# A trunk layer on one core: order of the x tiles, place of the gate row, and the filling of stick-breaking

## The chip, the core and the metric

The kernel runs on one core of a Trainium2 chip. The metric is device time in microseconds of one execution. Engines are named as in the profile: TensorE (PE, with its weight loads as PEld), VectorE (DVE), ScalarE (ACT), GpSimd (POOL) and SyncE (SP), whose queue issues the DMAs of this kernel.

## The reference

One layer with D = S = 1024, batch 1, float32. `h` feeds three groups of heads (mLSTM: 4 heads of 96; sliding window: 6 heads of 64 with 2 key/value heads; stick-breaking: 4 heads of 64), and their gated results go through `w_out`:

```python
mod = c_act @ w_mod + b_mod                       # c_act = silu(c)
shift, scale, gate = jnp.split(mod, 3, axis=-1)
h = rmsnorm(x, g_pre) * (1.0 + scale) + shift
proj = h @ w_in
(mu, mv, mi, mf, mz, aq, ak, av, az, sq, sk, sv, sz) = jnp.split(proj, OFFSETS, axis=-1)
y_m = mlstm_branch(mu, mv, mi, mf, ...) * silu(mz)
y_a = swa_branch(aq, ak, av, a_sinks) * silu(az)
y_s = stickbreak_branch(sq, sk, sv) * silu(sz)
y = concatenate([y_m, y_a, y_s]) @ w_out
x + gate * rmsnorm(y, g_post)
```

Stick-breaking, for queries `t` and keys `s < t`: `a = exp(log_sigmoid(z) + suffix)`, where `suffix` sums `log_sigmoid(-z)` over the keys between `s` and `t`, and the result is `a @ v`.

## The kernel before

Each large float32 product is made of three matmuls: both factors are split into a high part (rounded to the format that TensorE takes at full rate) and a low rest, and high x high, high x low and low x high are summed. Names with `h` and `l` at the end (`hh`/`hl`, `wh_d`/`wl_d`, `ah`/`al`) are such parts; ScalarE mostly makes the high part (a cast) and VectorE or GpSimd the low one (a subtraction).

The stages, in the order of TensorE:

- **x tiles** (0 to 34 us). Eight tiles of 128 tokens. For each, `x_sq` squares and sums on ScalarE (`junk`), `x_var` makes 1/rms (VectorE, then GpSimd, `rstd`), `x_scale` scales the tile, and `x_turn` transposes it on TensorE (`xps`, two groups of four) and copies the groups to `xT`. `mod_rows(k)` multiplies `silu(c)` with the modulation weights of one k slice (`mr`), `mod_sum(k)` turns the row into columns (`mps`, `sh`, `sc`), `mod_h(k, n)` makes `hh` and `hl` for one half of the tokens, and `mu_w(k)` splits a slice of the `mu` weights (`wmuh`, `wmul`).
- **mu** (22 to 72): `mu_mm(k, n)`, nine matmuls for one slice k of D and one half n of the tokens. The first, (0, 0), stands between the x tiles; from (0, 1) on they follow each other.
- **ptmif** (72 to 106): projection to the mLSTM's values and gates, by tokens.
- **gate chain** (106 to 151): `gmps` multiplies the two query and key matrices of the mLSTM (`wqk_s`) into one; then a chain of small transposes (`gtr`) with VectorE and ScalarE work between them (`fx`, `cm`, `mp`, `em`, `tcol`). Between the transposes, `fill(n)` issues n matmuls of the projections that are due anyway: `pd`, a transposed projection with weights `w_d` (48 matmuls to a tile of outputs), and `ptav`, the sliding window's values (24 to a tile of tokens, `vsh`/`vsl`, stored to `d_v`). `GF` holds the four counts, and `fill.through(I_AQ)` issues all that is left of `ptav`.
- **the gate row**: `gate_row` computes `gacc`, 32 instructions on VectorE over eight loads of 512 KB (`wg`, two buffers); `gate_sum` sums it over the partitions on TensorE (`gbps`, two halves) and writes the row `gbc`, which only the last stage of the kernel reads.
- **mLSTM** (about 175 to 244), chunk by chunk, with `cuh` (the convolution's result by heads), `mbc` (stabilizers, broadcast by a DMA), `qps`/`q`/`q1`, `kps` and `sps` (the scores).
- **sliding window** (244 to 331), with keys `ka` and values `va` loaded back from memory.
- **stick-breaking** (331 to 452): 40 steps `(h, pair, g)`; each transposes (`s_t`, tile `tp`), issues `SF[1]` fill matmuls on average, and three steps later multiplies with the values (`s_pv`, tile `ops`, one bank for the two quads of a head). `z`, `sg`, `pr` are the scores, the factors and their running products; `ys` collects the result.
- **the last projections and w_out** (452 to 569).

The order on TensorE is that of the code. For the x tiles the other engines and SyncE too follow the code; from the first slices of `mu` on a scheduler orders them, with the priorities that `tc.high_priority` gives. PSUM for fills has two banks, so a `ptav` tile can start when the evacuation of the tile before the last is done. At most eight DMAs of SyncE are under way: each waits for the landing of the one eight places ahead of it.

Of the kernel before, what the change touches and what calls it, by code (L numbers as in the profile page):

```python
# [13 lines left out]
ALU = mybir.AluOpType  # L14
# [17 lines left out]
C_CW, C_CB, C_NG, C_SKIP, C_SINK = 32, 44, 47, 50, 53  # L32
NCOLS = 59

EVD = (0, 1, 2, 3, 4)
WPRI, EPRI = 400, 200
GF = (48, 48, 48, 20)
PM = 12
MF = (12, 5, 5, 4)
AF_ = (4, 5, 4)  # L40
NPOOL = 3
SF = (6, 6.6, 2)
SL = 3
SGB = 8

# [2 lines left out]
def trunk(ctx: ExitStack, tc, x, w_ss, w_gate, rows, cols, w_mu, w_mif, w_dm, w_av, wqk, bif, alibi, w_out,  # L48
# [98 lines left out]
    def x_sq(i):  # L147

        junk = xp.tile([P, D], F32, tag="junk", bufs=1, name=f"junk{i}")
        ss, v, r = (sp.tile([P, 1], F32, tag=z, bufs=4, name=f"{z}{i}") for z in ("ss", "var", "rstd"))  # L150
        A.activation(junk, xt_[i], AF.Square, accum_out=ss)
        xs_[i] = (ss, v, r)

    def x_var(i):
        ss, v, r = xs_[i]
        V.tensor_scalar(out=v, in0=ss, scalar1=1.0 / D, scalar2=EPS, op0=ALU.mult, op1=ALU.add)
        G.tensor_tensor(out=r, in0=v, in1=mhalf[:, 0:1], op=ALU.pow)

    def x_scale(i):
        if i == NT - 1:  # L160
            A.mul(xt_[i], xt_[i], xs_[i][2])
        else:
            V.tensor_scalar(out=xt_[i], in0=xt_[i], scalar1=xs_[i][2], scalar2=None, op0=ALU.mult)

    def x_turn(i):
        for g in range(2):
            ps = sps.tile([P, 512], F32, tag="b", name=f"xps{i}_{g}")
            for q in range(4):
                k = g * 4 + q
                T.transpose(ps[:, q * P:(q + 1) * P], xt_[i][:, k * P:(k + 1) * P], ident)  # L170
            dst = xT[:, g * 4:(g + 1) * 4, i * P:(i + 1) * P]
            src = ps.rearrange("p (a b) -> p a b", a=4)
            if g == 1 and i in EVD:
                V.tensor_copy(dst, src)
            else:
                A.copy(dst, src)
# [74 lines left out]
    V.tensor_tensor(out=csil, in0=csil, in1=col[:, C_C:C_C + KT], op=ALU.mult)  # L251
    V.tensor_copy(csil32, csil.unsqueeze(2).to_broadcast([P, KT, 32]))
    V.tensor_scalar(out=col[:, C_BSC:C_BSC + KT], in0=col[:, C_BSC:C_BSC + KT], scalar1=1.0, scalar2=None, op0=ALU.add)
    x_sq(0)
    x_var(0)
    x_sq(1)
    x_scale(0)
    x_var(1)
    for i in range(NT):
        if i == 4:  # L260
            mod_rows(0)
            mod_sum(0)
            mod_h(0, 0)
        if i + 1 < NT:
            x_scale(i + 1)
        if i + 2 < NT:
            x_sq(i + 2)
            x_var(i + 2)
        if i == 4:
            mu_w(0)  # L270
        x_turn(i)
        if i == 4:
            mod_load(3)
            mu_load(3)
            mu_mm(0, 0)
        if i == NT - 2:
            mod_rows(1)
    mod_h(0, 1)
    mu_w(1)
    xstk.close()  # L280
    tw_stk = ExitStack()
    tw = pool("tw", side="right", stack=tw_stk)
# [244 lines left out]
    def gate_row():  # L527
        gacc = gp_.tile([P, D], F32, name="gacc")
        rowb = gp_.tile([P, 2, D], F32, name="rowb")
        load(rowb, rows.partition_broadcast(P))  # L530
        for s_ in range(4):
            a = gacc[:, s_ * 256:(s_ + 1) * 256]
            for q in range(2):
                w = gp_.tile([P, 4, 256], F32, tag="wg", bufs=2, name=f"wg{s_}_{q}")
                load(w, w_gate[s_][:, 4 * q:4 * q + 4, :])
                for i in range(4):
                    c = csil[:, 4 * q + i:4 * q + i + 1]
                    if q + i == 0:
                        V.tensor_scalar(out=a, in0=w[:, 0, :], scalar1=c, scalar2=None, op0=ALU.mult)
                    else:  # L540
                        V.scalar_tensor_tensor(out=a, in0=w[:, i, :], scalar=c, in1=a, op0=ALU.mult, op1=ALU.add)  # L541
# [125 lines left out]
    def m_qk(c):  # L667
# [5 lines left out]
        A.copy(d["q1"], heads(qps[0:MD, :], MH))
# [518 lines left out]
```

## Time and profile before

| | us |
|---|---|
| runs | 572.18, 572.54, 575.24 (median 572.54) |
| profiled execution | 571.31 |
| its span | 569.5 |
| TensorE busy | 533.2 (94%) |
| VectorE busy | 342.4 (60%) |
| ScalarE busy | 252.1 (44%) |
| GpSimd busy | 222.0 (39%) |

The mean granted clock of TensorE is 0.975. In 40 equal slices of 14.2 us, the profile gives the busy share of TensorE and the clock, both in tenths:

```profile
PE   4899999499997999999999999999999899999995
PEclk9699999989999999999999998999999999999998
```

The dips are the x tiles (slices 1 and 2), the stretch around 107 (slice 8), the entry of the mLSTM (slice 13) and the beginning and end of stick-breaking. In a row of the timeline stand the start, the duration, the engine, the line, the operation with its output and inputs, a count, and in brackets how long the engine stood idle before it and what ended that. In a row of windows stand the stretch, its length, the busy time (and instructions) of TensorE, its weight loads, VectorE, ScalarE and GpSimd, the granted clock, the DMA share and GB/s. In a list of waits stand the total, the number of times and the longest.

### The profile page before, as it was taken

What the parts mean: (1) busy time and instruction counts of PE and PEld (TensorE: products, weight loads), DVE (VectorE), ACT (ScalarE), POOL (GpSimd) and SP (SyncE); (2) the same over time, 40 slices, a digit from 0 to 9 for tenths busy, and PEclk for the clock granted to TensorE, in tenths of its full rate; (3) what the DMA queues carried; (4) which work ended last, traced back from release to release, by engine and by line L of the source; (5) the groups of instructions that cost most, each with busy time, mean ns of one, the idle gap of its engine ahead of it and who ended that gap; (6) DMA issues with size and microseconds to landing.
All of it is one profiled execution on the core that took longest, in us unless ns stands there. A gap on an engine that the chain in (4) does not pass through costs nothing.

```text
span 569.5 us, 8566 instructions
## 1 busy us (share of the span) xinstructions
PE 533.2 (94%) x2953; PEld 455.7 (80%) x2953; DVE 342.4 (60%) x768; ACT 252.1 (44%) x575; POOL 222.0 (39%) x208
## 2 busy tenths in 40 slices
PE   4899999499997999999999999999999899999995
PEld 3577799489996999888788777888888788888884
DVE  4467599664213677759888568786878443107232
ACT  5554433133012332336787677676766442104110
POOL 2344877321103243405534356566747253101000
PEclk9699999989999999999999998999999999999998
DMA  8973282545366945579964368548221369305421
GB/s 310 374 251 121 58 313 75 160 149 157 85 150 192 231 135 166 150 181 292 260 193 149 103 169 220 185 118 242 76 73 56 103 238 389 139 1 197 173 74 74
DMA packets 63659, 96.57 MB, mean 170 GB/s; under 512 B 17600, under 2 KB 36992, under 8 KB 63488
## 3 DMA queue, kind: packets, MB, share of 16 engines
q1 hardware_dynamic: 63616, 96.03, 53.7%
q8 instruction: 23, 0.38, 0.3%
q14 instruction: 20, 0.16, 0.1%
HBM read 69.24 MB, written 25.20 MB: 166 GB/s over the span
## 4 chain that ended last, share of the span: by engine, by line
PE 68%; DVE 12%; ACT 6%; DMA 5%; issue 4%; SPq 2%; POOL 2%; DVEq 0%; POOLq 0%; ACTq 0%
PE pd L360 22%; PE mu L237 6%; PE ptav L386 6%; PE op L1109 5%; PE op L1108 5%; PE op L1107 5%; DVE cu L508 3%; ACT zb L846 3%; SPq L65 2%; PE tp L993 2%; DVE gacc L541 2%; DMA xt<-in_x_dram 2%; DVE zb L856 2%; PE z L962 1%; PE ops L1012 1%
## 5 line engine op out<-in xcount | busy, mean ns | idle before, releaser
L360 PE MATMUL pd<-hh,wh_d 128*128 128x512 f32 x256 | 71.9, 407 | 0.0
L360 PE MATMUL pd<-hh,wl_d 128*128 128x512 f32 x256 | 71.7, 402 | 0.0
L360 PE MATMUL pd<-hl,wh_d 128*128 128x512 f32 x256 | 71.1, 402 | 0.0
L360 PEld LDWEIGHTS pd<-hh,wh_d 128*128 128x128 f32 x256 | 47.6, 194 | 8.3
L360 PEld LDWEIGHTS pd<-hl,wh_d 128*128 128x128 f32 x256 | 46.9, 191 | 8.4
L360 PEld LDWEIGHTS pd<-hh,wl_d 128*128 128x128 f32 x256 | 46.5, 190 | 8.2
L1107 PE MATMUL op<-woh,hh 128*128 128x512 f32 x128 | 50.6, 396 | 0.0
L1108 PE MATMUL op<-woh,hl 128*128 128x512 f32 x128 | 50.6, 396 | 0.0
L1109 PE MATMUL op<-wol,hh 128*128 128x512 f32 x128 | 50.6, 396 | 0.0
L303 POOL TENSOR_TENSOR wl_d<-w_d,wh_d 128x512 fp32r<-128x512 f32 x32 | 44.8, 1422 | 14.4 <-ACT wh_d L301 12.1
L981 POOL TENSOR_TENSOR sg<-sg,pr 128x512 f32<-128x512 f32 (+1 forms) x32 | 33.1, 1038 | 25.5 <-DVE pr L979 21.4
L72 DVE TENSOR_TENSOR al<-tp,ah 128x512 fp32r<-128x512 f32 (+2 forms) x56 | 27.6, 495 | 20.5 <-ACT ah L71 20.3
L856 POOL TENSOR_SCALAR zb<-zb,mx 128x256 f32<-128x256 f32 (+1 forms) x24 | 21.6, 911 | 41.9 <-DVE mx L853 11.3
L71 ACT CAST ah<-tp 128x512 fp32r<-128x512 f32 (+2 forms) x56 | 24.4, 436 | 28.0 <-PE tp L993 21.6
L1120 ACT ACTIVATE sj<-op 128x512 f32<-128x512 f32 x16 | 9.5, 598 | 61.3 <-PE op L1109 58.8
L1124 POOL TENSOR_TENSOR st<-st,mhalf 128x1 f32<-128x1 f32 x8 | 4.4, 554 | 67.3 <-DVE st L1123 44.9
L1108 PEld LDWEIGHTS op<-woh,hl 128*128 128x128 f32 x128 | 24.0, 188 | 5.9
L1109 PEld LDWEIGHTS op<-wol,hh 128*128 128x128 f32 x128 | 24.0, 188 | 5.8
L1107 PEld LDWEIGHTS op<-woh,hh 128*128 128x128 f32 x128 | 24.0, 188 | 5.8
L846 ACT ACTIVATE zb<-zb,mx 128x256 f32<-128x256 f32 (+1 forms) x48 | 23.2, 485 | 8.3 <-DVE mx L836 6.7
L979 DVE TENSOR_TENSOR_SCAN pr<-z,mzero 128x128 f32<-128x128 f32 (+3 forms) x32 | 25.4, 814 | 2.3 <-ACT z L970 1.9
L993 PE MATMUL tp<-ident,sg 128*128 128x128 f32 x144 | 23.0, 277 | 1.9 <-POOL sg L981 1.8
(248 smaller groups left out, 1350.3 us busy)
## 6 DMA issues: line engine op xcount, KB each, us to landing
wm<-in_w_ss_dram SPq DMA_DIRECT2D x16, 512.0 KB, 7.6
w_d<-in_w_dm_dram SPq DMA_DIRECT2D x16, 512.0 KB, 4.3
xt<-in_x_dram SPq DMA_DIRECT2D x8, 512.0 KB, 7.8
wg<-in_w_gate_dram SPq DMA_DIRECT2D x8, 512.0 KB, 4.6
wo<-in_w_out_dram SPq DMA_DIRECT2D x8, 512.0 KB, 5.3
xr<-in_x_dram SPq DMA_DIRECT2D x8, 512.0 KB, 4.7
out_dram<-ot SPq DMA_DIRECT2D x16, 256.0 KB, 2.3
hh<-d_yh SPq DMA_DIRECT2D x12, 256.0 KB, 6.3
```

What stands on the lines that cost most here:

```text
L72: e_lo.tensor_tensor(out=dst_l, in0=src, in1=dst_h.bitcast(F32), op=ALU.subtract)
L237: T.matmul(mu_acc[j][n], w[:, cs], h[:, k, t], start=(k == 0 and w is wh and h is hh), stop=(k == KT - 1 and h is hl))
L303: G.tensor_tensor(out=wl[:, a:b], in0=z[:, a:b], in1=wh.bitcast(F32)[:, a:b], op=ALU.subtract)
L360: T.matmul(ps, w[:, k, :], h[:, k, t], start=(k == 0 and w is wh and h is hh), stop=(k == KT - 1 and h is hl))
L386: T.matmul(ps[:, 0:self.N], h[:, k, t], w[:, k % 2, :], start=(k == 0 and q == 0), stop=(k == KT - 1 and q == 2))
L846: A.activation(z, z, AF.Exp, bias=nm[:, h:h + 1], accum_out=sm[:, h:h + 1])
L856: (G if h >= 6 - NPOOL else V).tensor_scalar(out=z, in0=z, scalar1=sm[:, h:h + 1], scalar2=None, op0=ALU.mult)
L981: (G if w > 256 else V).tensor_tensor(out=sg[:, 0:w], in0=sg[:, 0:w], in1=pr[:, 1:w + 1], op=ALU.mult)
L993: T.transpose(tp[:, bb, ti * P:(ti + 1) * P], attn[h, i, b // 4][:, (b % 4) * P:(b % 4 + 1) * P], ident)
L1107: T.matmul(o, hh[:, k, t], woh[:, k, cs], start=(k == 0), stop=False)
L1108: T.matmul(o, hl[:, k, t], woh[:, k, cs], start=False, stop=False)
L1109: T.matmul(o, hh[:, k, t], wol[:, k, cs], start=False, stop=(k == KT - 1))
```

## The change

It has five parts. (1) The x tiles are worked in two halves of four: all of tiles 0 to 3, then modulation and `mu_mm(0, 0)`, then tiles 4 to 7. All scalings and all second copies of a tile go to VectorE. (2) `gate_row` stands behind the gate chain instead of ahead of it, with four `wg` buffers in a pool of its own; `GF` goes from (48, 48, 48, 20) to (40, 24, 36, 0), and `gate_sum` stands behind the last `ptav`. (3) ScalarE's copy to `q1` has a priority. (4) `SF[1]`, the fill matmuls per step of stick-breaking, goes from 6.6 to 5.8. (5) The last head's second quad of `ops` has another bank than its first.

```diff
@@
 C_CW, C_CB, C_NG, C_SKIP, C_SINK = 32, 44, 47, 50, 53
 NCOLS = 59
 
-EVD = (0, 1, 2, 3, 4)
 WPRI, EPRI = 400, 200
-GF = (48, 48, 48, 20)
+GF = (40, 24, 36, 0)
 PM = 12
 MF = (12, 5, 5, 4)
 AF_ = (4, 5, 4)
 NPOOL = 3
-SF = (6, 6.6, 2)
+SF = (6, 5.8, 2)
 SL = 3
 SGB = 8
 
@@
         G.tensor_tensor(out=r, in0=v, in1=mhalf[:, 0:1], op=ALU.pow)
 
     def x_scale(i):
-        if i == NT - 1:
-            A.mul(xt_[i], xt_[i], xs_[i][2])
-        else:
-            V.tensor_scalar(out=xt_[i], in0=xt_[i], scalar1=xs_[i][2], scalar2=None, op0=ALU.mult)
+        V.tensor_scalar(out=xt_[i], in0=xt_[i], scalar1=xs_[i][2], scalar2=None, op0=ALU.mult)
 
     def x_turn(i):
         for g in range(2):
@@
                 T.transpose(ps[:, q * P:(q + 1) * P], xt_[i][:, k * P:(k + 1) * P], ident)
             dst = xT[:, g * 4:(g + 1) * 4, i * P:(i + 1) * P]
             src = ps.rearrange("p (a b) -> p a b", a=4)
-            if g == 1 and i in EVD:
+            if g == 1:
                 V.tensor_copy(dst, src)
             else:
                 A.copy(dst, src)
@@
     V.tensor_tensor(out=csil, in0=csil, in1=col[:, C_C:C_C + KT], op=ALU.mult)
     V.tensor_copy(csil32, csil.unsqueeze(2).to_broadcast([P, KT, 32]))
     V.tensor_scalar(out=col[:, C_BSC:C_BSC + KT], in0=col[:, C_BSC:C_BSC + KT], scalar1=1.0, scalar2=None, op0=ALU.add)
-    x_sq(0)
-    x_var(0)
-    x_sq(1)
-    x_scale(0)
-    x_var(1)
-    for i in range(NT):
-        if i == 4:
-            mod_rows(0)
+    for i0 in (0, 4):
+        x_sq(i0)
+        x_var(i0)
+        x_sq(i0 + 1)
+        x_scale(i0)
+        x_var(i0 + 1)
+        if i0:
+            mu_mm(0, 0)
+        for i in range(i0, i0 + 4):
+            if i + 1 < i0 + 4:
+                x_scale(i + 1)
+            if i + 2 < i0 + 4:
+                x_sq(i + 2)
+                x_var(i + 2)
+            if i == 3:
+                mod_rows(0)
+                mu_w(0)
+            if i == NT - 1:
+                mod_rows(1)
+            x_turn(i)
+        if i0 == 0:
             mod_sum(0)
             mod_h(0, 0)
-        if i + 1 < NT:
-            x_scale(i + 1)
-        if i + 2 < NT:
-            x_sq(i + 2)
-            x_var(i + 2)
-        if i == 4:
-            mu_w(0)
-        x_turn(i)
-        if i == 4:
             mod_load(3)
             mu_load(3)
-            mu_mm(0, 0)
-        if i == NT - 2:
-            mod_rows(1)
     mod_h(0, 1)
     mu_w(1)
+    mod_sum(1)
+    mod_h(1, 0)
     xstk.close()
     tw_stk = ExitStack()
     tw = pool("tw", side="right", stack=tw_stk)
@@
     for k in range(KT):
         if k > 0:
             mu_mm(k, 0)
-        if k + 1 < KT:
+        if 0 < k < KT - 1:
             mod_sum(k + 1)
             mod_h(k + 1, 0)
         if k + 2 < KT:
@@
         for s_ in range(4):
             a = gacc[:, s_ * 256:(s_ + 1) * 256]
             for q in range(2):
-                w = gp_.tile([P, 4, 256], F32, tag="wg", bufs=2, name=f"wg{s_}_{q}")
+                w = gw.tile([P, 4, 256], F32, tag="wg", bufs=4, name=f"wg{s_}_{q}")
                 load(w, w_gate[s_][:, 4 * q:4 * q + 4, :])
                 for i in range(4):
                     c = csil[:, 4 * q + i:4 * q + i + 1]
@@
                     else:
                         V.scalar_tensor_tensor(out=a, in0=w[:, i, :], scalar=c, in1=a, op0=ALU.mult, op1=ALU.add)
         return gacc, rowb
-
-    gacc, rowb = gate_row()
 
     def gate_sum():
 
@@
     V.tensor_copy(tcol, tp4[:, 0:96])
     acol, wscol, emcol = tcol[:, 0:32], tcol[:, 32:64], tcol[:, 64:96]
     mg_stk.close()
+    gw_stk = ExitStack()
+    gw = pool("gw", stack=gw_stk)
+    gacc, rowb = gate_row()
     fill(GF[3])
+    fill.through(I_AQ)
     gate_sum()
-    fill.through(I_AQ)
+    gw_stk.close()
     gstk.close()
     tw_stk.close()
     mpad_stk.close()
@@
         for h in range(MH):
             T.matmul(qps[0:MD, h * P:(h + 1) * P], gm[:, h, :], kc[:, h, :], start=True, stop=True)
         d["q1"] = mw.tile([MD, MH, P], F32, tag="q1", name=f"q1_{c}")
-        A.copy(d["q1"], heads(qps[0:MD, :], MH))
+        with tc.high_priority(offset=WPRI + 50):
+            A.copy(d["q1"], heads(qps[0:MD, :], MH))
         if c > 0:
             d["q2"] = mw.tile([MD, MH, P], F32, tag="q2", name=f"q2_{c}")
             V.tensor_tensor(out=d["q2"], in0=heads(qps[0:MD, :], MH), in1=d["wib"], op=ALU.mult)
@@
     def s_pv(h, pair, g):
         quad, vh = pair // 2, sh_[h][3]
         if pair % 2 == 0 and g == pair:
-            op_t[h, quad] = bank("o", (5,), f"ops{h}_{quad}")
+            op_t[h, quad] = bank(f"o{quad}", (5 if h < SH - 1 or quad == 0 else 4,), f"ops{h}_{quad}")
         ops = op_t[h, quad]
         ah, al = op_t.pop((h, pair, g))
         for bb in range(2):
```

SyncE's queue around `wqk_s` (the mLSTM's query and key weights, 96x768 as loaded). Before:

```order
L65 DMA bi<-in_bif_dram 32x2
L65 DMA w_av_1143<-in_w_av_dram 128x768
L65 DMA w_d_1568<-in_w_dm_dram 128x1024
L65 DMA w_d_1660<-in_w_dm_dram 128x1024
L65 DMA w_d_1963<-in_w_dm_dram 128x1024
L65 DMA wg_0_1074<-in_w_gate_dram 128x1024
L65 DMA wg_1_1080<-in_w_gate_dram 128x1024
L65 DMA wg_0_1086<-in_w_gate_dram 128x1024
L65 DMA wqk_s<-in_wqk_dram 96x768
L65 DMA wg_1_1092<-in_w_gate_dram 128x1024
L65 DMA wg_0_1098<-in_w_gate_dram 128x1024
```

and after:

```order
L64 DMA w_av_1092<-in_w_av_dram 128x768
L64 DMA rowb<-in_rows_dram 128x2048
L64 DMA w_d_1572<-in_w_dm_dram 128x1024
L64 DMA w_d_1664<-in_w_dm_dram 128x1024
L64 DMA w_d_1967<-in_w_dm_dram 128x1024
L64 DMA wqk_s<-in_wqk_dram 96x768
L64 DMA w_av_1099<-in_w_av_dram 128x768
L64 DMA w_av_1106<-in_w_av_dram 128x768
L64 DMA d_akh<-sh_ak_0_1145 128x512
```

`wqk_s` moved ahead of all eight `wg` loads, of which five stood ahead of it; they now come among the stores of `vsh` and `vsl`.

The entry of the mLSTM, again on SyncE, from the last tiles of `ptav` (`vsh`, `vsl`) on. Before:

```order
L65 DMA d_v<-vsh_1502 768x1x64
L65 DMA d_v<-vsl_1503 768x1x64
L65 DMA bias_a<-in_alibi_dram 128x1536
L65 DMA cuh_1553<-cu 96x256
L65 DMA d_v<-vsh_1533 768x1x64
L65 DMA d_v<-vsl_1534 768x1x64
L65 DMA cuh_1553<-cu 32x256
L65 DMA cuh_1553<-cu 64x256 x2
L65 DMA cuh_1553<-cu 32x256
L65 DMA cuh_1553<-cu 96x256
L65 DMA mbc_1560<-d_m 128x512
L65 DMA mbc_1650<-d_m 128x512
```

and after:

```order
L64 DMA ka_2262<-d_akh 64x2x256
L64 DMA d_v<-vsh_1527 768x1x64
L64 DMA ka_2262<-d_akh 64x2x256
L64 DMA ka_2262<-d_akl 64x2x256
L64 DMA d_v<-vsl_1528 768x1x64
L64 DMA ka_2262<-d_akl 64x2x256
L64 DMA va_2264<-d_v 128x2x256
L64 DMA cuh_1557<-cu 96x256
L64 DMA cuh_1557<-cu 32x256
L64 DMA cuh_1557<-cu 64x256 x2
L64 DMA cuh_1557<-cu 32x256
L64 DMA cuh_1557<-cu 96x256
```

The five loads of `ka` and `va` moved from behind the first stabilizers (`mbc`) to ahead of `cuh`; the two `mbc` follow behind these rows as before.

VectorE at the end of `ptav`. Before:

```order
L622 COPY tcol<-gtr_1420 128x96
L72 TENSOR_TENSOR vsl_1432<-ptav_1396,vsh_1431 128x384
L553 TENSOR_TENSOR gbc<-gbps_1455,rowb 128x512
L553 TENSOR_TENSOR gbc<-gbps_1459,rowb 128x512
L72 TENSOR_TENSOR vsl_1472<-ptav_1437,vsh_1471 128x384
L72 TENSOR_TENSOR vsl_1503<-ptav_1477,vsh_1502 128x384
L72 TENSOR_TENSOR vsl_1534<-ptav_1508,vsh_1533 128x384
L423 SCALAR_TENSOR_TENSOR sl_aq_0_1601<-pd_0_1570,sh_aq_0_1600 128x512
L661 TENSOR_TENSOR e_1562<-tcol,mbc_1560 128x512
```

and after:

```order
L540 SCALAR_TENSOR_TENSOR gacc<-wg_1_1361,csil,gacc 128x256 x2
L538 TENSOR_SCALAR gacc<-wg_0_1367,csil 128x256
L540 SCALAR_TENSOR_TENSOR gacc<-wg_0_1367,csil,gacc 128x256 x3
L540 SCALAR_TENSOR_TENSOR gacc<-wg_1_1373,csil,gacc 128x256
L550 TENSOR_TENSOR gbc<-gbps_1534,rowb 128x512
L540 SCALAR_TENSOR_TENSOR gacc<-wg_1_1373,csil,gacc 128x256
L71 TENSOR_TENSOR vsl_1528<-ptav_1502,vsh_1527 128x384
L540 SCALAR_TENSOR_TENSOR gacc<-wg_1_1373,csil,gacc 128x256 x2
L550 TENSOR_TENSOR gbc<-gbps_1538,rowb 128x512
L422 SCALAR_TENSOR_TENSOR sl_aq_0_1605<-pd_0_1574,sh_aq_0_1604 128x512
L662 TENSOR_TENSOR e_1566<-tcol,mbc_1564 128x512
```

The sum over partitions (`gbps`, then `gbc`) moved behind the last `ptav`, and between the two `gbc` stand three of the last `gacc` and the last `vsl`; `sl_aq` is the evacuation of the next projection.

## The prediction

> **What bounds it now.** I read the waits of TensorE first, then the timeline around each, then the windows for the granted clock (the column behind POOL). TensorE is busy nearly everywhere, so only its idle time, its half-clock time and reordered work can move the end.
>
> ```profile
> PE gmps L566 <- DMA wqk_s<-in_wqk_dram: 7.7, 1, 7.7
> ...
> PE xps L170 <- ACT xT L176: 2.2, 1, 2.2
> PE sps L689 <- ACT q L673: 3.7, 1, 3.7
> PE tp L993 <- POOL sg L981: 1.8, 1, 1.8
> ...
> PE ops L1011 <- DVE ys L1018: 1.5, 1, 1.5
> PE mu L237 <- ACT wmuh L71: 1.0, 1, 1.0
> ```
>
> The longest wait is one for a 288 KB weight, `wqk_s`. SyncE's queue shows why it is late:
>
> ```profile
> 100.34 8.45 SPq L65 DMA_DIRECT2D wg<-in_w_gate_dram  x3
> 108.88 0.38 SPq L65 DMA_DIRECT2D wqk_s<-in_wqk_dram  x1
> ```
>
> Three gate-row loads stand ahead of it; with two `wg` buffers each waits until VectorE has used up an older one. And the idle time is followed by a half clock:
>
> ```profile
> 106.00:114.00 8.00, 0.30 (x2) 0.00 (x0) 5.34 (x11) 0.55 (x2) 2.15 (x2) 0.84 0.55 163
> 114.00:116.00 2.00, 1.96 (x10) 1.89 (x11) 1.35 (x4) 0.36 (x1) 0.00 (x0) 0.50 0.23 66
> 116.00:118.00 2.00, 2.00 (x6) 1.54 (x5) 1.40 (x3) 0.13 (x1) 0.00 (x0) 0.50 0.75 242
> 118.00:120.00 2.00, 2.00 (x10) 1.65 (x9) 1.31 (x3) 0.00 (x0) 0.00 (x0) 0.93 0.69 168
> ```
>
> **Gate row behind the gate chain.** `wqk_s` goes ahead of all `wg` loads. It then waits only for its buffer, held by the convolution on GpSimd, which is done at 91.48 + 8.54 = 100.0:
>
> ```profile
> 91.48 8.54 POOL L513 TENSOR_TENSOR cu<-cu,cusg 128x1024 f32<-128x1024 f32 x3 [2.25 <-ACT cusg L512]
> ```
>
> Before, it took 5.0 from its issue at 108.88 until TensorE went on at about 114, so now it lands near 105, while TensorE is still in the `ptmif` projection (until 106.2). The 7.75 go. With them goes the half clock: 0.0 idle leaves no reason for it, and 114.0 to about 118.2, 4.2 us at half speed, did 2.1 us of work: another −2.1. Together −9.85. Bounds: −7.75 if the slow window comes all the same; −10.5 if the 0.6 of later small waits went too.
>
> The shorter fills (40, 24, 36) must still cover the gate chain. The rates by the starts of matmuls in unbroken rows, 16 `ptav` from first to last and two rows of eight `pd`:
>
> ```profile
> 161.77 0.34 PE L386 MATMUL ptav<-wl_av,hh 128*128 128x384 f32 x1
> ...
> 164.39 0.34 PE L386 MATMUL ptav<-wl_av,hh 128*128 128x384 f32 x1
> 171.82 1.98 PE L360 MATMUL pd<-hh,wl_d 128*128 128x512 f32 x8
> 173.63 1.98 PE L360 MATMUL pd<-hl,wh_d 128*128 128x512 f32 x8
> ```
>
> A `ptav` takes 2.62 / 15 = 0.175, a `pd` 1.81 / 8 = 0.226. So they are 28 `pd` and 12 `ptav`, 8.5 us, over a chain that took VectorE 6.15 from `fx` to `cm` (by its timeline); 24 `ptav`, 4.2, over about 1.4; 36, 6.3, over about 1.9. All cover, so 0. Taking 32 `gacc` instructions off VectorE ahead of the chain also lets `fx` start when its input is there.
>
> Behind the chain about 120 `ptav` are left, 21 us of TensorE. In them VectorE has to do 32 `gacc` and the last `vsl`. The price of one `gacc` is in two rows:
>
> ```profile
> 105.05 3.39 DVE L541 SCALAR_TENSOR_TENSOR gacc<-wg,csil,gacc 128x256 f32<-128x256 f32 x3
> ...
> 121.91 2.05 DVE L541 SCALAR_TENSOR_TENSOR gacc<-wg,csil,gacc 128x256 f32<-128x256 f32 x4 [1.39 <-DMA wg<-in_w_gate_dram]
> ```
>
> 0.51 with GpSimd idle, 1.13 beside GpSimd's `wl_av`. In the stretch in question GpSimd does little:
>
> ```profile
> 140.00:150.00 10.00, 10.00 (x59) 9.44 (x59) 2.67 (x9) 1.76 (x5) 0.00 (x0) 1.00 0.38 85
> ```
>
> So I take 0.51: 16.3 us, with five `vsl` of 0.56 19.1, and some 4 us before the first load lands: 23 against 21. The order of VectorE at the end says the same: the last `gacc` stand behind the first `gbc`, which waits for the first `gbps`. From there `gbps1` waits 0.69 (`gbc`) + 0.51 + 0.56 (`vsl`) + 2 x 0.51, about 2.9 us, with nothing on TensorE to fill it, since 48 `pd` of the next tile are queued behind. The pair of `gbps` itself (four records in 1.88 us) is only moved.
>
> What follows is the entry of the mLSTM:
>
> ```profile
> 154.97 0.69 DVE L553 TENSOR_TENSOR gbc<-gbps,rowb 128x512 f32<-128x512 f32 x1 [0.17 <-PE gbps L552]
> 164.56 1.75 PE L360 MATMUL pd<-hh,wh_d 128*128 128x512 f32 x7
> 165.28 0.56 DVE L72 TENSOR_TENSOR vsl<-ptav,vsh 128x384 fp32r<-128x384 f32 x1 [3.64 <-ACT vsh L71]
> 172.20 1.26 SPq L65 DMA_DIRECT2D mbc<-d_m  x2
> 177.29 1.03 DVE L661 TENSOR_TENSOR e<-tcol,mbc 128x512 f32<-128x512 f32 x1 [0.23 <-DMA mbc<-d_m]
> 181.64 1.16 PE L689 MATMUL sps<-q,cuh 96*128 96x128 f32 x8 [3.67 <-ACT q L673]
> ...
> d_v<-vsl SPq DMA_DIRECT2D x2, 192.0 KB, 4.8
> ...
> va<-d_v SPq DMA_DIRECT2D x1, 256.0 KB, 7.5
> ...
> d_v<-vsl SPq DMA_DIRECT2D x8, 192.0 KB, 2.5
> ```
>
> (The last three rows are the time to landing, of this stretch and of the whole run.) Before, `ptav` ended at 164.74 and `sps` started 16.9 later, 4.35 after the second `mbc` had let VectorE start `e`. ScalarE takes `q` behind the second `e`, so `sps` hangs on `mbc`. Now `ka` and `va` loads (five, 768 KB) stand ahead of `cuh` and `mbc`. With T for the end of `ptav`: the last `vsl` is done at T + 0.9 + 0.69 + 0.51 + 0.56 = T + 2.7, its store lands at about T + 5.2 (2.5 by the median of all eight such stores; 4.8 by the two in this stretch), `va` at T + 12.7 (7.5), and `mbc`, behind it in the same queue, about 4.3 later, T + 17.0; plus 4.35 is T + 21.4. TensorE alone would be there at T + 18.2: 4.8 for the gate sum with its wait, 10.9 for 48 `pd`, 2.5 for `qps`, `kps`, five `pd` and the hand-over. The other end is T + 23, with the store at 4.8. I take 21.4, since the queue's order is fixed and every load in it was late in these rows. That is +4.5 against 16.9; the 1.88 of `gbps` now lie in it rather than ahead of T, so **+2.6** net (−0.6 to +4.2). Loads that left the mLSTM's body give nothing: TensorE had no wait on them there.
>
> **The x tiles.** Before, ScalarE squared tile 4 (a load) ahead of copying tile 2:
>
> ```profile
> 12.75 0.49 PE L170 MATMUL xps<-ident,xt 128*128 128x128 f32 x3
> 13.82 1.06 ACT L151 ACTIVATE junk<-xt 128x1024 f32<-128x1024 f32 x1 [2.86 <-DMA xt<-in_x_dram]
> 15.49 0.79 PE L170 MATMUL xps<-ident,xt 128*128 128x128 f32 x4 [2.25 <-ACT xT L176]
> 16.21 1.08 PE L201 MATMUL mr<-wm,csil 128*32 128x256 f32 x8
> ...
> 22.49 1.65 PE L237 MATMUL mu<-hh,wmuh 128*128 128x512 f32 x3 [0.98 <-ACT wmuh L71]
> ...
> 31.96 0.96 PE L237 MATMUL mu<-hh,wmuh 128*128 128x512 f32 x3 [0.16 <-ACT hh L223]
> ```
>
> Now nothing of tile 4 stands ahead of tiles 0 to 3, and `mr` comes right after tile 2's transposes: 16.21 − 13.24 = 3.0 earlier. `wmuh` is cast ahead, so its 1.0 goes. The transposes of tile 4 move from ahead of the first `mu` to behind it; that is an even exchange. The second `mu` chunk, from which TensorE is full without a break, starts at about 28 instead of 31.96: **−4.0**. Tile 7's scaling on VectorE (0.75 by the same instruction) instead of ScalarE (1.16) and three more copies there (0.68 each against 0.57) are on engines that idle most of that time, but VectorE's queue then carries tiles and modulation alike; −2.5 is the poor end. The good end comes from the clock:
>
> ```profile
> 16.00:26.00 10.00, 8.47 (x38) 5.38 (x37) 5.59 (x12) 4.75 (x10) 4.05 (x5) 0.50 1.03 417
> ...
> 343.00:347.00 4.00, 4.00 (x13) 3.04 (x12) 2.88 (x4) 2.57 (x6) 1.91 (x2) 0.57 1.10 303
> ```
>
> The nine `mu` took 4.0 at half speed; at full speed (0.23 each) they take 2.1. If the clock holds, −5.9. I leave it half, since a wait of 1.84 us (the 1.8 on `sg` in the list of waits, ended at 342.44) was enough for the last row, and some waits stay. [...]
>
> **`q1` with a priority.** The row order of ScalarE around each `q1` is unchanged: 0.
>
> **Stick-breaking.** Forty steps put 6.6 `pd` each between one step's transposes and its values; now 5.8. The supply ran out with about 9 steps to go, so 31 x 0.8, about 25 matmuls or 5.7 us, move from the body to the tail. The tail was not full:
>
> ```profile
> 444.00:446.00 2.00, 1.07 (x9) 0.79 (x7) 1.45 (x3) 1.94 (x4) 0.11 (x1) 1.00 0.00 0
> 446.00:448.00 2.00, 1.42 (x12) 1.42 (x13) 1.24 (x3) 0.98 (x3) 1.27 (x2) 1.00 0.00 0
> ```
>
> 0.93 + 0.58 = 1.5 us of idle, which is the wait for the value bank that `ys` must free; the second bank takes that wait away too, so it isn't counted again. With small gaps that the rows show as busy I take 1.9 recovered. In the body nearly no idle shows, but a fill stretch can stand as busy over a wait:
>
> ```profile
> 438.55 1.85 PE L360 MATMUL pd<-hh,wl_d 128*128 128x512 f32 x7
> ```
>
> Seven at 0.226 are 1.58; they cover 1.87 till the next row (440.42). A step is thus partly set by the chain of VectorE and GpSimd. Of the 5.7 I take about 60% as real: −3.4. Sum: −3.4 + 5.7 − 1.9 = **+0.4**, from −1.8 (all real) to +3.8 (none). Of the wait of 1.8 on `sg` at 342 and its half clock I expect no change: GpSimd's queue decides it.
>
> **Sum.** −9.85 + 2.6 − 4.0 + 0.4 = −10.8; 571.31 − 10.8 = 560.5 for the profiled execution. The median of the runs, 572.54, lies 1.2 above it; I go halfway and predict 561.
>
> **Rivals.** *Gate row as the bound (slower).* If each `gacc` takes the 1.13 of the slow row, the 32 cost 19.8 more than counted, in a stretch that VectorE fills already: `vsl` come late, TensorE waits for projection banks, `gbps1` waits: 560.5 + 19.8 = 580. It decides from 0.51 + 10.8 / 32 = 0.85 each. GpSimd idle in 140 to 150 speaks against it. [...] Chance 0.05. *Stick-breaking set by its chain:* nothing of the 5.7 is real, 564; against it stands that 1.58 of the 1.87 us between two steps above were matmuls at full rate: 0.15. *TensorE-bound entry of the mLSTM:* 557.5, if `va` and `mbc` overlap: 0.2. *Little gain in the x stage:* 562 to 563: 0.15. Forecast as it stands: 0.42. *No change:* the wait moves to another operand of `gmps` (its `cu` is done at 100, which speaks against it): 0.03.
>
> Within 0.5%, about what a measurement of this kernel can tell from no change, means 569.7 to 575.4. Faster by more: 0.92, same 0.03, slower 0.05. The terms' ends added up give 553 to 569; 8 in 10 lie in 555.5 to 566.5.
>
> **What would show it.** `gmps` without a wait and no half clock near 105 to 110; `gbps1` waiting 2 to 4 us; `sps` 18 to 23 after the last `ptav`; the second `mu` chunk at 27 to 29.5; stick-breaking within −2 to +4 us, with `ops` not waiting for `ys`. A `gacc` of 0.85 or more, or TensorE waiting for `vsl` amid `ptav`, would make the forecast wrong.

## The result and the profile after

The changed kernel takes 564.08 us (median of four runs, 563.44 to 564.55), the kernel before 573.07 in the same comparison: a ratio of 0.9837 (95% interval 0.9806 to 0.9867). The profiled execution took 563.44 with a span of 561.3, 8.2 less than the 569.5 of before. It is faster, inside the range, and 3 us slower than the forecast of 561. That the sum came so near is partly luck: one term was not in it at all and another came out worse than forecast, and two that came out better hid them. The kernel before varies between executions: in the sessions of the experiments 49 of them lie between 566.3 and 575.1 us, and one of 600.9, with a granted clock of 0.843, is left out of the comparisons.

Where TensorE stood in the two profiled executions, in us from the start of the span, by the starts of the groups (the end of `ptav` is the start of what follows it):

| | before | after | difference |
|---|---|---|---|
| second chunk of `mu` starts | 31.96 | 26.37 | −5.6 |
| first `ptmif` | 71.7 | 66.0 | −5.7 |
| `gmps` | 114.04 | 106.3 | −7.7 |
| end of `ptav` | 164.6 | 153.0 | −11.6 |
| first `sps` | 181.64 | 173.02 | −8.6 |
| last `qps` of the mLSTM | 238.4 | 227.9 | −10.5 |
| first `z` of stick-breaking | 330.71 | 320.26 | −10.5 |
| last `ops` | 451.63 | 443.42 | −8.2 |

The 5.7 us won by the x tiles are gone again where `ptmif` ends: 34.5 us of `ptmif` before, 40.3 after. The list of TensorE's waits of the changed kernel (engine and line, what was waited for, us in total, times, longest):

```profile
PE xps L166 <- DVE var L155: 8.9, 4, 7.4
PE gbps L549 <- DVE gacc L540: 3.2, 1, 3.2
PE ops L1013 <- DVE ys L1020: 3.1, 4, 1.1
PE ptmif L385 <- ACT igf L447: 3.0, 1, 3.0
PE tp L995 <- POOL sg L983: 2.1, 1, 2.1
PE ao L881 <- DVE ya L894: 1.7, 3, 0.9
PE mu L233 <- ACT hh L219: 1.6, 1, 1.6
```

The wait of `gmps` on `wqk_s`, 7.7 us, is gone, as is that of `sps` on `q`, 3.7. New are 3.0 in `ptmif`, which no step of the prediction had, and 3.2 at the gate sum, which it had as 2.9. The new wait in `ptmif` ends with ScalarE's copy of `igf`, the second half of a tile's evacuation. ScalarE there (start, duration, line, operation; idle time before it and what ended it):

```profile
84.42 2.26 ACT L511 ACTIVATE cusg<-cu 128x1024 f32<-128x1024 f32 x2 [4.82 <-DVE cu L507]
89.03 1.06 ACT L511 ACTIVATE cusg<-cu 128x1024 f32<-128x1024 f32 x1 [2.35 <-POOL cu L512]
90.00 0.46 ACT L446 COPY v<-ptmif 128x384 f32<-128x384 f32 x1
90.36 0.17 ACT L447 COPY igf<-ptmif 128x8 f32<-128x8 f32 x1
```

Three sigmoids of the convolution (`cusg`, two buffers) stand in a row, and the evacuation of `ptmif` tile 3 behind them. The third waits until GpSimd has used the first one's buffer. Before, the evacuation of tile 3 (the row at 92.57) stood ahead of the third sigmoid:

```profile
91.60 1.06 ACT L512 ACTIVATE cusg<-cu 128x1024 f32<-128x1024 f32 x1 [0.20 <-DVE cu L508]
92.57 0.46 ACT L447 COPY v<-ptmif 128x384 f32<-128x384 f32 x1
...
94.98 1.06 ACT L512 ACTIVATE cusg<-cu 128x1024 f32<-128x1024 f32 x1 [1.89 <-POOL cu L513]
```

With the change, TensorE needs that bank at 87.6 and gets it at 90.58, and then runs slowly (windows of the changed kernel: stretch, length, busy time of TensorE, its weight loads, VectorE, ScalarE, GpSimd, then the granted clock, DMA share, GB/s):

```profile
84.00:90.00 6.00, 3.60 (x21) 3.27 (x19) 2.78 (x3) 3.09 (x4) 4.44 (x2) 0.98 0.26 87
90.00:96.00 6.00, 5.42 (x17) 5.42 (x18) 0.09 (x1) 0.98 (x5) 3.64 (x2) 0.50 0.17 49
96.00:102.00 6.00, 6.00 (x34) 6.00 (x33) 0.00 (x0) 0.55 (x2) 0.00 (x0) 0.95 0.00 0
```

17 matmuls in six us at half clock against 34 in the next six: 3.0 of waiting and about 2.9 of half speed are the 5.8 that `ptmif` lost. In f2 and f3, two variants below with the same wait of 3.0, `ptmif` took 39.1, which leaves about 1.6 for the half speed: this loss is 4.6 to 5.8.

In the x tiles the clock stayed whole, where it had been 0.50 from 16 to 26:

```profile
10.00:16.00 6.00, 4.50 (x42) 3.47 (x40) 4.73 (x11) 3.26 (x8) 1.56 (x2) 1.00 1.03 418
16.00:26.00 10.00, 8.48 (x73) 6.30 (x77) 6.44 (x14) 7.38 (x14) 3.50 (x5) 1.00 1.03 417
```

The entry of the mLSTM, on TensorE:

```profile
153.00 1.02 PE L549 MATMUL gbps<-gacc,ones 128*128 128x512 f32 x2
157.22 1.28 PE L549 MATMUL gbps<-gacc,ones 128*128 128x512 f32 x2 [3.19 <-DVE gacc L540]
157.75 3.99 PE L359 MATMUL pd<-hh,wh_d 128*128 128x512 f32 x8
161.58 1.99 PE L359 MATMUL pd<-hh,wl_d 128*128 128x512 f32 x8
...
173.02 1.11 PE L691 MATMUL sps<-q,cuh 96*128 96x128 f32 x8
```

The second `gbps` waits 3.19, and the eight `pd` behind it take 3.8 from start to start where the next eight take 1.8: the half clock again, 0.50 from 158.0 to 161.4.

In stick-breaking the wait for `ys` stands four times instead of once. VectorE's `ys` marks the end of each quad; the first, the sixth and the last of them before, and then after:

```profile
360.38 0.66 DVE L1018 TENSOR_TENSOR ys<-ops,otmp 64x512 f32<-64x512 f32 x1
...
439.71 0.65 DVE L1018 TENSOR_TENSOR ys<-ops,otmp 64x512 f32<-64x512 f32 x1
...
452.62 0.68 DVE L1018 TENSOR_TENSOR ys<-ops,otmp 64x512 f32<-64x512 f32 x1 [1.38 <-ACT otmp L1017]
```

```profile
350.43 0.66 DVE L1020 TENSOR_TENSOR ys<-ops,otmp 64x512 f32<-64x512 f32 x1
...
427.51 0.66 DVE L1020 TENSOR_TENSOR ys<-ops,otmp 64x512 f32<-64x512 f32 x1
...
444.40 0.68 DVE L1020 TENSOR_TENSOR ys<-ops,otmp 64x512 f32<-64x512 f32 x1 [0.77 <-ACT otmp L1019]
```

From the first `z` to the first `ys` it takes 30.2 instead of 29.7, from there to the sixth 77.1 instead of 79.3, and from there to the end 16.9 instead of 12.9: +2.2 in all.

### The profile page after: what moved, and what is told of

Read it like the earlier page. It is cut to its first block, busy times and chain, and to the rows that moved or that the text cites. A ratio compares the mean times of both kernels' runs of the same rounds, so it can differ in the third digit from the quotient of the medians.

```text
span 561.3 us, 8574 instructions
## 1 busy us (share of the span) xinstructions
PE 529.2 (94%) x2953; PEld 453.4 (81%) x2953; DVE 337.1 (60%) x772; ACT 251.2 (45%) x571; POOL 223.5 (40%) x208
## 4 chain that ended last, share of the span: by engine, by line
PE 74%; DVE 12%; ACT 7%; issue 2%; POOL 2%; DMA 1%; DVEq 0%; POOLq 0%; SPq 0%; ACTq 0%
PE pd L359 23%; PE ptav L385 6%; PE mu L233 6%; PE op L1111 5%; PE op L1110 5%; PE op L1109 5%; PE ptmif L385 3%; DVE cu L507 3%; ACT zb L848 3%; PE tp L995 2%; DVE pr L981 2%; DVE zb L858 2%; PE xps L166 2%; PE mr L197 1%; PE ops L1013 1%
## 5 line engine op out<-in xcount | busy, mean ns | idle before, releaser
L302 POOL TENSOR_TENSOR wl_d<-w_d,wh_d 128x512 fp32r<-128x512 f32 x32 | 46.3, 1469 | 12.9 <-ACT wh_d L300 12.9
L385 PE MATMUL ptmif<-wh_mif,hh 128*128 128x392 f32 x64 | 23.2, 362 | 3.0 <-ACT igf L447 3.0
```

Of the source, the lines that this page charges most:

```text
L302: G.tensor_tensor(out=wl[:, a:b], in0=z[:, a:b], in1=wh.bitcast(F32)[:, a:b], op=ALU.subtract)
L385: T.matmul(ps[:, 0:self.N], h[:, k, t], w[:, k % 2, :], start=(k == 0 and q == 0), stop=(k == KT - 1 and q == 2))
```

## The experiments

All times are medians; each ratio is to the kernel before, run on the same chip, whose medians lay between 570.2 and 573.1. Two variants are compared by a few tenths of a per cent at best, since most were not run beside each other and the clock does not fall to half at the same places in every execution (see the end).

| | us | ratio (95%) |
|---|---|---|
| the change | 564.08 | 0.9837 (0.9806 to 0.9867) |
| e1 evacuation ahead of the sigmoids | 557.62 | 0.9756 (0.9696 to 0.9816) |
| h1 third sigmoid buffer alone | 559.59 | 0.9808 (0.9774 to 0.9841) |
| e2 gate row alone | 567.10 | 0.9921 (0.9882 to 0.9959) |
| e3 x tiles alone | 566.58 | 0.9900 (0.9863 to 0.9937) |
| e4 stick-breaking alone | 574.35 | 1.0042 (1.0004 to 1.0081) |
| f1 24 `pd` ahead of the gate sum | 562.63 | 0.9851 (0.9787 to 0.9915) |
| f2 6.6 fills a step | 559.46 | 0.9810 (0.9734 to 0.9887) |
| f3 one bank for the last head | 562.45 | 0.9858 (0.9793 to 0.9923) |
| f4 e1 + f1 + f2 | 555.18 | 0.9740 (0.9659 to 0.9821) |
| g1 e1 + f2 | 554.59 | 0.9714 (0.9673 to 0.9756) |
| g2 g1 + 12 `pd` ahead of the gate sum | 554.36 | 0.9703 (0.9663 to 0.9743) |
| g3 g1 with 7.2 fills a step | 560.49 | 0.9809 (0.9760 to 0.9858) |

### The loss in `ptmif`: e1, h1

```diff
# e1: around the three sigmoids
+    order2.enter_context(tc.manual_schedule(engines={ET.Activation}))
+    fill(96 - 1)
+    for j in range(3):
-        sg = cvp.tile([P, S], F32, tag="sg", bufs=2, name=f"cusg{j}")
+        sg = cvp.tile([P, S], F32, tag="sg", bufs=3, name=f"cusg{j}")
...
     fill.through(1)
+    order2.close()
# h1: bufs=3 alone
```

> The changed kernel with one order on ScalarE altered: the evacuation of ptmif tile 3 stands ahead of the three cusg (sigmoids of the convolution), which get a third buffer. Theory: in the changed kernel the third cusg, which waits for GpSimd, holds that evacuation, TensorE waits 3.0 us for a projection bank and then runs some 6.5 us at half speed (another 3). Without it ptmif takes 34.5 us as before instead of 40.3: 5.5 to 6 us less than the changed kernel, about 558. Rival: the convolution itself is late and the wait moves to gmps (on wqk_s, issued only at 93.7 when the convolution is done): then gmps waits and less than 2.5 us is won, 561.5 or more.

> The changed kernel with a third buffer for cusg and nothing else: tile 3's evacuation stays behind all three cusg on ScalarE, but the third no longer waits for GpSimd to free the first one's buffer. Theory: the three then run from 84.4 to 87.9 without a break, the evacuation ends at about 88.5, and TensorE, which needs the bank at 87.6, waits 0.9 instead of 3.0; a wait that short brings no half clock, so 2.1 + about 3 of the 5.9 come back: 559. Rival: what counts is the order alone, and the half clock comes with a wait of 0.9 too: 562 to 563.

e1: 557.6 against an expected 558. TensorE has no wait left in `ptmif`, which takes 34.3 us (66.9 to 101.2), and the clock stays at 1.00:

```profile
84.00:90.00 6.00, 6.00 (x35) 6.00 (x35) 3.65 (x3) 4.17 (x7) 3.74 (x3) 1.00 0.24 87
90.00:96.00 6.00, 6.00 (x35) 6.00 (x34) 0.09 (x1) 0.55 (x2) 4.62 (x2) 1.00 0.16 49
```

The rival, a wait that moves on to `gmps`, falls: `gmps` follows `ptmif` at 101.2 without one. h1: 559.6 against an expected 559. The order is that of the changed kernel, but the sigmoids run through and the evacuation comes at 88.0 instead of 90.0:

```profile
84.64 3.46 ACT L511 ACTIVATE cusg<-cu 128x1024 f32<-128x1024 f32 x3 [4.82 <-DVE cu L507]
88.00 0.46 ACT L446 COPY v<-ptmif 128x384 f32<-128x384 f32 x1
...
84.00:90.00 6.00, 5.24 (x30) 4.92 (x29) 3.00 (x3) 4.07 (x7) 4.22 (x2) 1.00 0.25 87
```

About 0.8 us of idle is left and no half clock. So both halves of the loss are shown: a wait of 3.0 that comes from the order on ScalarE and from the buffer, and a half clock that comes with a wait of that length in all five profiles that have it (0.50 from 90 to 96 with the change, 0.59 from 96 to 102 in e2, `ptmif` rows of 0.53 us or more instead of 0.34 in f1, f2 and f3) and not with the one of 0.8 in h1 (1.00 from 84 to 102). The order alone, with two buffers, was not run.

### The parts alone: e2, e3, e4

e2 takes the parts of the diff that name `gate_row`, `gw`, `GF`, `gate_sum` and `fill.through`; e3 those of the x tiles and `mod_sum`; e4 `SF` and the bank.

> The kernel before with the gate row's part alone (gate row behind the chain, four wg buffers, fills 40, 24, 36, 0, gate sum behind the last ptav). Theory: it carries both the gain at gmps (7.75 of wait and 2.1 of half speed) and the loss in ptmif (about 5.9), because taking the gate row's instructions away makes the scheduler put all three cusg ahead of tile 3's evacuation; with 0.6 won around the mLSTM's entry that is about -4.6, 568.5. Rival: the loss in ptmif belongs to the x tiles' order; then ptmif keeps its 34.4 us here and the gain is about 10.4, 562.5.

> The kernel before with the x tiles' part alone. Theory: the mu projection starts and ends 5.7 us earlier, ScalarE keeps tile 3's evacuation ahead of the third cusg, and the late wqk_s load is as late relative to it as before, since its queue hangs on the convolution and on gacc, which start 5.7 earlier too: about -5.7, 567. Rival (the loss in ptmif belongs to the x tiles' order, or the wait at gmps ends at a fixed time): 0 to -1.5, 571.5 to 573.

> The kernel before with stick-breaking's part alone (5.8 fill matmuls a step and another bank for the last head's second quad). Theory from the two traces: the heads become 2.2 us shorter, the tail 4.0 longer, the start 0.5 longer: +2.2 us, about 575. Rival: the 2.2 us come from elsewhere in the changed kernel (other phases of the same stage, loads at other times); then 0 to +0.5, 573.

The list of TensorE's waits, one line from e2 and one from e3:

```profile
PE ptmif L386 <- ACT igf L448: 3.0, 1, 3.0
```

```profile
PE gmps L565 <- DMA wqk_s<-in_wqk_dram: 7.8, 1, 7.8
```

The loss in `ptmif` belongs to the gate row: it is in e2, where the x tiles are those of before, and not in e3. e2 wins 5.4 by the medians (4.6 was expected, 10.4 by the rival). What links the two is the scheduler's order. On VectorE one `gacc` stood among the nine multiply-adds of the convolution before; in e2 they are one row, and the third sigmoid moves ahead of tile 3's evacuation. VectorE before, and then in e2:

```profile
75.38 11.40 DVE L508 SCALAR_TENSOR_TENSOR cu<-mup,col,cu 128x1024 f32<-128x1024 f32 x6
86.70 1.38 DVE L539 TENSOR_SCALAR gacc<-wg,csil 128x256 f32<-128x256 f32 x1
88.00 4.70 DVE L508 SCALAR_TENSOR_TENSOR cu<-mup,col,cu 128x1024 f32<-128x1024 f32 x3
```

```profile
76.94 17.07 DVE L508 SCALAR_TENSOR_TENSOR cu<-mup,col,cu 128x1024 f32<-128x1024 f32 x9
```

That it is the missing `gacc`, and not the fill counts or buffers that e2 changes too, is read from these rows; no run took it out alone. e3 wins 5.9: the x tiles' whole gain reaches the end, because the late `wqk_s` comes as much earlier (its load is issued at 103.53 instead of 108.88). e4 loses 1.9 by the medians, 2.2 being expected; its heads have the same lengths as in the changed kernel (first to sixth `ys` 363.82 to 440.93, 77.1; last 457.85). By the medians the three parts alone add up to −9.4; the change measured −9.0 against the executions beside it.

### The gap at the gate sum: f1, f4, g2

```diff
     fill.through(I_AQ)
+    fill(24)          # g2: fill(12)
     gate_sum()
```

> The changed kernel with 24 of the next projection's pd matmuls (5.4 us) issued ahead of the gate sum instead of behind it. Theory: the second gbps waits 3.2 us with nothing to cover it, and the 3.2 us gap brings a window of half clock (the eight pd behind it take 3.8 us instead of 1.8): 3.2 + 1.9 = 5.1 less than the changed kernel, about 559. Rival: the mLSTM's entry is set by the loads of mbc behind the gate sum, which then starts later: sps waits for q instead, and less than 2 us is won, 562 or more.

> The changed kernel with all three: tile 3's evacuation ahead of the cusg (as in e1), 24 pd ahead of the gate sum, and 6.6 fills a step. If the three causes are separate: 6.5 + 5 + 2.5 less than the changed kernel, about 550. If the mLSTM's entry is set by mbc behind a later gate sum, 553 to 556.

> As g1, with 12 pd (2.7 us) ahead of the gate sum, not 24. With 24, the last cuh and both mbc stood in SyncE's queue behind the store of sh_aq's second half, and mbc landed 5 to 6 us later than in the changed kernel; with 12 that store stands behind mbc again. Theory: the wait of the second gbps falls to about 0.5, no half clock follows, and q waits only for mbc's chain: 1.5 to 3 less than g1, 550 to 551.5. Rival: mbc, which cannot be loaded before the gate sum, binds the entry all the same: no difference to g1.

f1: 562.6 instead of 559; my theory fell and the rival's time held, though by other waits than it named. The gap and the half clock are gone (the eight `pd` behind the gate sum take 2.3 instead of 3.8), but `qps` now waits 2.5 for `cuh` and `nps` 1.4, and the first `z` of stick-breaking starts no earlier than in the changed kernel (320.2 and 320.3). SyncE's queue shows the cause (start, duration, the load or store):

```profile
166.53 0.32 SPq L64 DMA_DIRECT2D d_aqh<-sh_aq  x1
166.89 0.53 SPq L64 DMA_DIRECT2D cuh<-cu  x1
167.53 0.54 SPq L64 DMA_DIRECT2D d_aql<-sl_aq  x1
168.11 0.95 SPq L64 DMA_DIRECT2D mbc<-d_m  x2
```

In the changed kernel it reads:

```profile
158.48 4.15 SPq L64 DMA_DIRECT2D cuh<-cu  x6
162.68 1.08 SPq L64 DMA_DIRECT2D mbc<-d_m  x2
166.04 0.32 SPq L64 DMA_DIRECT2D d_aqh<-sh_aq  x1
```

With 24 `pd` moved, the scheduler puts the last `cuh` and both `mbc` behind a store that waits for ScalarE, and `mbc` is issued 5.4 later. f4, which has this too, came out at 555.2, in the range of its second case. g2 puts `mbc` ahead of that store again, and still shows no gain over g1 (554.36 and 554.59). TensorE comes to `sps` 15.0 after the end of `ptav` (162.85 to 147.84, in the changed kernel 20.0) and then waits at `nps`, for `am`, the scores times `e`:

```profile
PE nps L719 <- DVE am L699: 2.1, 1, 2.1
```

VectorE, GpSimd and ScalarE work on `e` one after the other, and VectorE begins when `mbc` has landed. VectorE and GpSimd in g2:

```profile
162.85 1.33 DVE L668 TENSOR_TENSOR e<-tcol,mbc 128x512 f32<-128x512 f32 x1 [0.83 <-DMA mbc<-d_m]
...
162.35 2.96 POOL L302 TENSOR_TENSOR wl_d<-w_d,wh_d 128x512 fp32r<-128x512 f32 x2 [7.40 <-ACT wh_d L300]
165.27 1.28 POOL L750 TENSOR_TENSOR cu<-cu,col 128x384 f32<-128x384 f32 x1
166.51 1.55 POOL L669 TENSOR_SCALAR_AFFINE_SELECT e<-e 128x512 f32<-128x512 f32 x2
```

Three things ate the gain: `mbc` was issued 11.4 after the end of `ptav` instead of 9.7, GpSimd had `wl_d` and `cu` to do first and began `e` 2.3 after VectorE's part was done, and behind the wait of 2.1 the clock fell (0.74 from 168 to 172). In the changed kernel itself `e` does not bind: ScalarE had finished it at 169.70, and VectorE's `am` waited for `sps` until 174.17. So filling the gap was worth nothing in these variants because it moved the loads and the work on `e` too; what it would be worth with both left in place, or with `mbc` loaded ahead of the gate sum, wasn't tried. f4 and g1 differ only in the moved gate sum, and neither is faster beyond the scatter of the runs.

### Fills and bank: f2, f3, g1, g3

```diff
-SF = (6, 5.8, 2)
+SF = (6, 6.6, 2)      # f2; g3: 7.2
# f3, with SF as in the change:
-            op_t[h, quad] = bank(f"o{quad}", (5 if h < SH - 1 or quad == 0 else 4,), f"ops{h}_{quad}")
+            op_t[h, quad] = bank("o", (5,), f"ops{h}_{quad}")
```

> The changed kernel with 6.6 instead of 5.8 fill matmuls a step, the last head's second quad still in its own bank. Theory: fewer fills a step don't shorten the steps in proportion (waits for ys at the quads' change take their place) and lengthen the tail, so going back wins the 2 us that the stick-breaking part lost, and the bank takes up to 1.5 us of idle in the unfilled tail: 2 to 3.5 less than the changed kernel, 560.5 to 562. Rival: in the changed kernel's setting the count makes no difference, 563.5 to 564.5.

> The changed kernel with the last head's second quad in the same bank as its first. Theory: with fills up to the end of the stage the wait for ys at the last quad's change is about 1.0 us, as at the other heads' (1.1, 0.6 and 1.0): 0.5 to 1 more than the changed kernel, about 565. Rival: the fills there cover it: no difference.

> The changed kernel with tile 3's evacuation ahead of the cusg and 6.6 fills a step (bank part kept), the gate sum where the change put it. Theory: e1 (6.5) and f2 (4.6) are separate stages and add up: 553.0; then f4, 555.2 with the gate sum moved as well, gained nothing from moving it. Rival: they overlap somewhere, 555 or more, and moving the gate sum was neutral in f4.

> As g1, with 7.2 fills a step instead of 6.6. Theory: from 5.8 to 6.6 each fill moved into a step cost the step about half of its 0.226 us and saved the tail all of it; on that slope 7.2 wins another 1 to 2 us. Rival: the supply ends some 12 steps before the end, the unfilled steps wait for their own chain, and it is the same as g1 or up to 1.5 slower.

From the first `z` to the last `ops`, stick-breaking took 120.9 before (6.6 fills, one bank), 123.2 with the change (5.8, two), 119.3 in f2 (6.6, two) and 122.5 in f3 (5.8, one). These totals can't be subtracted as they are: behind the wait on `sg` near the beginning of the stage the clock fell to half before and with the change, and not in f2 and f3, which is worth about 1 us (from the first `z` to the first `ys` 29.7 before and 28.6 in f2 at 6.6 fills, 30.2 with the change and 29.3 in f3 at 5.8). From the sixth `ys` to the last it took 12.9, 16.9, 12.6 and 17.1 us in the same order, and from the first to the sixth 79.3, 77.1, 79.2 and 77.1. So the second bank is worth 0.2 to 0.4 at either count: at 6.6 fills the wait of 1.5 on `ys` goes, but a wait of `tp` of 1.5 on `al` takes its place. With the same bank, the fewer fills win about 2.2 between the first and the sixth `ys` and cost 4.2 to 4.3 behind it; compared at the same clock, they cost the whole stage 2.6 (the change against g1) to 2.9 (f3 against e2). f2 (559.5, under its range) therefore owes part of its gain over the change to the clock, and f3 (562.5 instead of 565) was not slower than the change, as its rival said.

g1, e1 and f2 together, comes to 554.6: 1.6 more than the plain sum, and the fastest but for g2, which is the same within the scatter. g3 fell from the slope that I had drawn, and further than its rival (5.9 slower than g1, 1.5 at most being expected). With 7.2 the supply is used up earlier, and the steps without it wait for their own chain (list of waits, and two windows near the end):

```profile
PE ops L1018 <- DVE ys L1025: 4.0, 4, 3.1
...
420.00:430.00 10.00, 7.59 (x45) 6.44 (x43) 7.40 (x14) 6.57 (x15) 5.70 (x6) 1.00 0.12 48
430.00:440.00 10.00, 8.27 (x57) 7.96 (x58) 5.66 (x12) 4.94 (x10) 3.18 (x3) 0.83 0.14 52
```

2.4 and 1.7 us of idle time and a dip in the clock. From the first to the sixth `ys` g3 takes 84.4 where g1 takes 79.3, about 1.0 more in each of the five quads, and from there to the last `ys` only 0.7 less (11.9 and 12.5), since few fills were left for that end in g1 already (16, in g3 4). Of the three counts tried with e1's order, 5.8 (e1, 557.6), 6.6 (g1) and 7.2 (g3), 6.6 is the fastest.

## Why the prediction was right, and where it was not

**Gate row, −9.85: right in itself (measured −9.8), with a cost that I had not seen.** The wait at `gmps` and its half clock went as forecast: `wqk_s` was issued at 93.67, when the convolution was done, and landed 3.0 later. The shorter fills covered the chain. From the first `ptmif` to the end of `ptav` it takes 5.9 less; 1.9 of that is the gate sum, which moved out, and 5.8 were lost in `ptmif`, which leaves −9.8 for the rest. The step that failed is the sentence that taking 32 `gacc` off VectorE "also lets `fx` start when its input is there": I priced what leaves that stretch as pure gain and looked at the order on SyncE, TensorE and VectorE, but not at ScalarE's in `ptmif`, where the same part of the change moved one evacuation. It cost 5.8 (e1, e2, h1), a term that the sum put at nothing.

**x tiles, −4.0: measured −5.6 (e3: −5.9).** The mechanism held: `mr` starts at 12.07 instead of 16.21, and `wmuh` waits no more. The size is the good end of the range, −5.9, which rested on the clock. With the wait of 2.25 gone, the longest left in that stretch is 1.6 (`mu` on `hh`), and the clock stayed at 1.00. I had left it at half because "some waits stay". That was not without ground: in f2, f3 and g3 some of the matmuls behind the same wait of 1.6 ran at the slow rate (`mu<-hl` rows of up to 0.63 to 0.64 us, at most 0.40 with the change).

**Entry of the mLSTM, +2.6: measured −0.8.** The gap came as forecast (3.19 against 2.9, whose terms add up to 2.8), and `sps` came 20.0 behind `ptav` against 21.4. Two clock windows were left out of the sum: one behind the gap, about +2.0, inside these 20.0, and one of before, behind the 3.67 that `sps` had waited, which is gone:

```profile
183.00:187.00 4.00, 4.00 (x20) 3.52 (x19) 1.64 (x3) 0.00 (x0) 0.68 (x1) 0.57 0.63 121
```

That is about the 1.8 by which the way from `sps` to stick-breaking got shorter. Counted from the start of what follows `ptav`, `sps` was 17.1 behind it before, and 20.0 − 17.1 − 1.9 − 1.8 = −0.8. The step that failed here is that `sps` hangs on `mbc`: `va` landed 9.4 behind the end of `ptav`, not 12.7, `e` was done 4.5 before it was needed, and TensorE's queue ended last. That is the rival of a TensorE-bound entry, to which I had given 0.2. It would have been at 18.2 by my count, and is at 20.0 with the slow stretch.

**Stick-breaking, +0.4: measured +2.2 (e4: +1.9).** The term that was mis-sized is the share of the body's saving that is real. Between the first and the sixth `ys` the traces have 25 fills less (182 and 157), 5.7 us, and they shortened the steps by 2.2, 40% against 60%; up to the first `ys` the fewer fills won nothing. The tail, with 23 fills more, grew by 4.0, near 5.7 − 1.9 = 3.8, but not for the reason given: of the 1.5 that the bank was to take away it took 0.2 to 0.4 (f2, f3).

**q1.** The order around each `q1` is unchanged; it was not run alone.

The terms as measured, −5.6 − 9.8 + 5.8 − 0.8 + 2.2 = −8.2, are the −8.2 of span. Against the forecast of −10.8 that is +5.8 and +1.8 on one side and −1.6 and −3.4 on the other. Of the rivals, the one by which the change would have been slower fell: `gacc` stayed at 0.51 (four in 2.05) and never held up TensorE amid `ptav`. Of the rival with nothing won in the steps of stick-breaking about half came true, and the one of the entry held. Two of the signs failed: the second `mu` chunk started at 26.4 (27 to 29.5 was said), and `ops` waited for `ys`.

## What to carry to other kernels

Where a scheduler orders the engines, work that leaves an engine's queue changes the order on others too: compare every engine's order over the whole stretch from which work is taken, and above all what stands ahead of a PSUM evacuation. Price each wait of TensorE with the slow clock that can come behind it, both the ones that go and the ones that come, and compare two variants stage by stage only where the clock was the same in both. Before filling a gap, look at what the fill moves on the other engines: here it moved loads and GpSimd's work behind other things, and the filled gap won nothing.

## What the runs showed of the hardware

In windows cut where it changes, the granted clock was 1.00 or 0.50 in the profiles of before and after. Amid the kernel it was half from 15.87 to 26.11, 111.45 to 118.27, 183.13 to 186.54 and 343.55 to 346.96 us before (10.2, 6.8, 3.4 and 3.4 us), and from 89.73 to 96.56, 158.00 to 161.41 and 332.07 to 335.49 with the change (6.8, 3.4 and 3.4). Counted in the length of the shortest, 3.41 us, their starts lie 28, 21 and 47 apart before, and 20 and 51 with the change.

Each of them begins during a wait of TensorE or at most 1.5 us behind its end: waits of 2.25, 7.7, 3.67 and 1.84 us before, and 3.0, 3.19 and 2.1 with the change. Behind the other waits that followed the first transposes, up to 1.5 (`ops` on `ys`) before and up to 1.6 (`mu` on `hh`) with the change, the clock was 1.00, but for those inside such a stretch.

Whether a wait brings such a stretch differs between executions. Behind the wait of 1.8 on `sg` it came before and in f4 and g1 (29.6 to 29.7 us from the first `z` to the first `ys`), but not in f2 and g2 (28.6). Behind the 1.6 of `mu` on `hh` it came in f2, f3 and g3 (`mu<-hl` rows of up to 0.63 to 0.64 us), but not with the change nor in e1, e3, f1, f4, g1 and g2 (at most 0.41). Behind the waits of 2.5 on `cuh` in f1 and f4 it did not come (the five `pd` there took 1.24 and 1.23 from start to start, 0.25 each). No run shows what decides it. The same wait of 3.0 in `ptmif` cost 5.8 with the change and 4.6 in f2 and f3.

The profile before shows a `pd`, with rounded factors, as one record of 0.39 us (128x512), and a `gbps` of the same size, whose factors aren't rounded, as two of 0.59. Of SyncE's 322 DMAs none was issued before the one eight places ahead had landed, in the profile of before or of after.

The kernel before scatters with it: of the 49 executions, the 21 with a mean granted clock of 0.973 or less took 573.4 on average, and the 16 with 0.981 or more 569.1.
